# Probabilities times values in full fp32 on half the TensorE columns, in a hybrid decoder trunk

## The chip, the core and the metric

The kernel runs on one core of a Trainium2 chip. The metric is device time in microseconds (us) of one execution. A profile is one execution taken by the hardware profiler, with the same kernel; its times carry the names and lines of the kernel's code.

## What is computed

Two decoder layers over 512 tokens of width 1024. The first layer is a convolution module and a SwiGLU feed-forward part; then one shared set of keys and values is projected; the second layer is sliding-window attention over them and a second feed-forward part. Cut to the attention, where `probs` times `v_band` is what the change touches:

```python
def banded_sink_attention(q, k, v, sinks, rel_bias):
    # 16 query heads, 4 key/value heads of 64, 4 blocks of 128 queries;
    # a block sees its own 128 keys and the 128 before
    s = jnp.einsum('bnqhgd,bnkhd->bnhgqk', qb, k_band) * (HEAD_DIM ** -0.5)
    s = jnp.where(mask, s + bias, NEG_INF)
    m = jnp.maximum(jnp.max(s, axis=-1, keepdims=True), sink)
    p = jnp.exp(s - m)
    probs = p / (jnp.sum(p, axis=-1, keepdims=True) + jnp.exp(sink - m))
    o = jnp.einsum('bnhgqk,bnkhd->bnqhgd', probs, v_band)
    return o.reshape(B, S, N_HEADS * HEAD_DIM)
```

## The kernel before

Activations lie with features on the 128 partitions and tokens along the free dimension. Weights come in pieces of 128 x 1024 floats, in the order of a plan written out at the start: DMA on the SP queue (line 188), then ScalarE writes a rounded high part (`whi`, line 204) and VectorE the rest (`wlo`, line 205). `mm3` (lines 259 to 265) multiplies two such split operands with three matmuls in the fp32r type: high times high, high times low, low times high. The first projection (line 630) alone multiplies unsplit fp32 tiles, of 256 columns.

Around the attention the work stands like this. While the last of layer 0's feed-forward part runs, the normalised inputs of keys, values and queries are made. `kq` takes the keys, split. The values come out of the banks `vb`, 128 tokens at a time, are scaled by the token's norm (line 980), and are split into two tiles `vq` that were set to zero by two memsets on GpSimd (line 950). In `vq` each pair of key/value heads has four slots of 64 columns, [v0, 0, 0, v1]: slots 0 and 1 are the first side's values with zeros beside them, slots 2 and 3 are zeros with the second side's values.

`unit` is the attention of one pair of key/value heads (`gp`), one half of their query heads (`jp`) and one block of 128 queries (`n`); there are 16 units, of one key block (n = 0) or two. A unit has these steps, parted by `yield`:

- scores (line 1024): 12 matmuls, alternately with the upper and the lower 64 rows of the array, into two banks; one small matmul (line 1019) stands ahead of them so that they are issued in that order; VectorE adds the bias and takes the extreme (line 1027);
- exponentials on ScalarE (line 1034), a reciprocal on VectorE (line 1036), the scaling on GpSimd (line 1038);
- for each key block four transposes on TensorE into a bank (line 1046), from which ScalarE writes the high part `pth` (line 1049) and VectorE the rest `ptl` (line 1050);
- probabilities times values, P·V (lines 1053 to 1059): for each key block and each side `g` one `mm3` of 256 columns into the bank `po`. Its stationary operand is 128 columns of `vq`, one side's 64 and the zeros, so the two sides add up in one accumulation over all 128 partitions: 6 matmuls per key block, 168 in all, on lines 263 to 265;
- `po` is split into the output tiles (lines 1064 and 1065).

`pipeline` staggers the units, and its steps are set between the matmuls of the query projections (`query`) and of the first half of the output projection. On top of that a scheduler that simulates the engines' times decides the order in which each engine gets its instructions, so the order in the code isn't that of the engines: a P·V group may stand broken up between projections and transposes.

Tiles come from rotating pools: 8 banks of PSUM; 11 wide buffers `quad`, of which `vq` holds two; two each of `pth` and `ptl`.

Of the kernel before, what the change touches and what calls it, by code (L numbers as in the profile page):

```python
# [10 lines left out]
F32 = mybir.dt.float32  # L11
F32R = mybir.dt.float32r
AF = mybir.ActivationFunctionType
ALU = mybir.AluOpType
# [3 lines left out]
P = 128  # L18
# [8 lines left out]
HD = 64  # L27
NBLK = S // P
BAND = 2 * P
# [121 lines left out]
def hybrid_trunk(ctx: ExitStack, tc: tile.TileContext, xT, W, prm_in, wdw_in, sinks, relb, onehot, fin, out):  # L151
    nc = tc.nc
    cpool = ctx.enter_context(tc.tile_pool(name="const", bufs=1))
    quads = ctx.enter_context(tc.tile_pool(name="quads", bufs=11))
# [8 lines left out]
    def uid(s):  # L163
        ctr[0] += 1
        return f"{s}{ctr[0]}"

    def bank():
        return ps.tile([P, 512], F32, tag="bank", name=uid("bank"))

    def quad(dt=F32R):  # L170
        return quads.tile([P, 4, 512], dt, tag="quad", name=uid("quad"))

    def temp():
        return tmp.tile([P, 512], F32, tag="tmp", name=uid("tmp"))

    def f32(ap):
        return ap.bitcast(F32)
# [81 lines left out]
    def mm3(out, w, x, start, stop):  # L259
        if w[1] is None:  # L260
            nc.tensor.matmul(out, w[0], x, start=start, stop=stop)
            return
        nc.tensor.matmul(out, w[0], x[0], start=start, stop=False)  # L263
        nc.tensor.matmul(out, w[0], x[1], start=False, stop=False)  # L264
        nc.tensor.matmul(out, w[1], x[0], start=False, stop=stop)  # L265
# [141 lines left out]
    def split(dst, src):  # L407
        nc.scalar.copy(dst[0], src)  # L408
        nc.vector.tensor_sub(dst[1], src, f32(dst[0]))
# [504 lines left out]
    at = attn.enter_context(tc.tile_pool(name="attn", bufs=2))  # L914
# [25 lines left out]
    if True:  # L940
# [4 lines left out]

        xkv = x["kv"]
        kq = quads.tile([P, 2, 2, 512], F32R, tag="quad", name="kq")
        vq = [quads.tile([P, 4, 2, 4, HD], F32R, tag="quad", name=uid("vq")) for _ in range(2)]
        for v in vq:
            nc.gpsimd.memset(f32(v), 0.0)  # L950
        kb = [bank() for _ in range(2)]
        for half in range(2):
            whi, wlo = get("kv", 0, half)
# [6 lines left out]
        vb = [bank() for _ in range(4)]  # L960
        for half in range(2):
# [7 lines left out]
            if half == 0:  # L969
                rs_bc = rms.step2()  # L970
                rs = rms.rs
                for m in range(2):
                    t = temp()
# [2 lines left out]
        flush()  # L976
        rate[0] = 0
        for n in range(4):
            t = temp()
            nc.vector.tensor_scalar(t[:, 0:256], vb[n][:, 0:256], rs[:, n:n + 1], None, op0=ALU.mult)  # L980
            split([v[:, n, :, 0:4:3, :] for v in vq], t[:, 0:256].rearrange("p (a g c) -> p a g c", a=2, g=2))

        qs, os_ = {}, {}

# [21 lines left out]
        def unit(gp, jp, n):  # L1006
            qt = slice(n * P, (n + 1) * P)
            k0 = max(n - 1, 0) * P
            nk = 1 if n == 0 else 2
            w = nk * P  # L1010
            rows = [slice(HD * g, HD * (g + 1)) for g in range(2)]
            heads = [gp * 8 + g * 4 + 2 * jp + e for g in range(2) for e in range(2)]
            sc = at.tile([P, 4, 1 + BAND], F32, tag="sc", name=uid("sc"), bufs=3)
            sinks4 = sk.rearrange("p (a g j e) -> p a g j e", a=2, g=2, j=2)[:, gp, :, jp, :]
            nc.gpsimd.tensor_copy(sc[:, :, 0].rearrange("p (g e) -> p g e", g=2), sinks4)
            m4 = small.tile([P, 4], F32, tag="m4", name=uid("m4"))
            pbs = [bank().rearrange("p (a b) -> p a b", a=2) for _ in range(2)]

            mm = nc.tensor.matmul(pbs[1][0:1, 0, 0:1], ones_c, ones_c, start=True, stop=True)
            for e in range(2):  # L1020
                for a, b in ((0, 0), (0, 1), (1, 0)):
                    for g in range(2):
                        with tc.issue_after(mm.ins):
                            mm = nc.tensor.matmul(pbs[g][:, e, :], qs[gp, jp][rows[g], 2 * a + e, qt],  # L1024
                                                  kq[rows[g], b, gp, k0:k0 + BAND], start=a + b == 0, stop=a == 1)
            for u, hd in enumerate(heads):
                nc.vector.tensor_tensor_reduce(
                    sc[:, u, 1:1 + w], pbs[u // 2][:, u % 2, 0:w], bias[:, hd, BAND - w:BAND],
                    op0=ALU.add, op1=ALU.min, scale=1.0, scalar=sk[:, hd:hd + 1],
                    accum_out=m4[:, u:u + 1])  # L1030
            yield
            sm = small.tile([P, 4], F32, tag="sm", name=uid("sm"))
            for j in range(4):
                nc.scalar.activation(sc[:, j, 0:1 + w], sc[:, j, 0:1 + w], AF.Exp, bias=m4[:, j:j + 1],
                                     scale=-1.0, accum_out=sm[:, j:j + 1])
            nc.vector.reciprocal(sm, sm)  # L1036
            for j in range(4):
                nc.gpsimd.tensor_scalar(sc[:, j, 1:1 + w], sc[:, j, 1:1 + w], sm[:, j:j + 1], 0.0,  # L1038
                                        op0=ALU.mult, op1=ALU.add)
            yield  # L1040
            yield
            pts = []
            for kb_ in range(nk):
                pt = bank()
                for j in range(4):
                    nc.tensor.transpose(pt[:, j * P:(j + 1) * P], sc[:, j, 1 + kb_ * P:1 + (kb_ + 1) * P], ident)  # L1046
                hi = at.tile([P, 512], F32R, tag="pth", name=uid("pth"), bufs=2)
                lo = at.tile([P, 512], F32R, tag="ptl", name=uid("ptl"), bufs=2)
                nc.scalar.copy(hi, pt)
                nc.vector.tensor_sub(lo, pt, f32(hi))  # L1050
                pts.append((hi, lo))
            yield
            po = bank()[:, 0:BAND]
            for kb_ in range(nk):
                blk = k0 // P + kb_
                for g in range(2):
                    vs = [v[:, blk, gp, 2 * g:2 * g + 2, :].rearrange("p a c -> p (a c)") for v in vq]
                    mm3(po, vs, [pt[:, g * BAND:(g + 1) * BAND] for pt in pts[kb_]],
                        kb_ == 0 and g == 0, kb_ == nk - 1 and g == 1)
            if n == 0:  # L1060
                os_[gp, jp] = quad()
            hi, lo = (os_[gp, jp][:, 2 * a:2 * a + 2, qt] for a in range(2))
            src = po.rearrange("p (j q) -> p j q", j=2)
            nc.scalar.copy(hi, src)
            nc.vector.tensor_sub(lo, src, f32(hi))
            yield

        def pipeline():
            units = [unit(gp, jp, n) for gp in range(2) for jp in range(2) for n in range(NBLK)]
            for t in range(len(units) + 4):  # L1070
                for d in (4, 3, 1, 0):
                    if 0 <= t - d < len(units):
                        next(units[t - d])
                        if d == 1:
                            next(units[t - d])
                yield
# [129 lines left out]
```

## Time and profile before

| | |
|---|---|
| median of 3 runs | 1104.37 us (1103.89 to 1104.98) |
| the profiled execution | 1105.28 us, span of its instructions 1103.5 us |
| mean granted TensorE clock | 0.995 of full speed |
| TensorE matmuls busy | 1088.4 us, 99% of the span |
| TensorE weight loads busy | 931.5 us, 84% |
| VectorE, ScalarE, GpSimd busy | 662.7, 506.1, 335.3 us |

In the profile PE is TensorE's matmuls, PEld its weight loads, DVE is VectorE, ACT ScalarE, POOL GpSimd, SP the engine whose queue issues most DMAs. A row of a group gives line, engine, operation, output and inputs by the program's names, shape, count; then busy time in us and the mean ns of one; then the engine's idle time ahead of them and what ended it. Durations of matmuls include the pipeline's latency, so in a dense stream they overlap, and the distance from start to start is what one costs. An fp32 matmul is shown as two pieces.

### The profile page before, as it was taken

Reading aid. Unit: us, or ns where it says so; the run is one execution under the profiler, and the core shown is the slowest. Engines: PE = TensorE matmul, PEld = TensorE weight load, DVE = VectorE, ACT = ScalarE, POOL = GpSimd, SP = SyncE. Lnnn points to the kernel's source line nnn. Section 1 sums busy time; section 2 is a strip of 40 time slices with the busy share of each in tenths; the row PEclk is TensorE's granted clock in tenths of the full one; section 3 lists DMA queues with packets and bytes.
Section 4 is the critical chain, followed back from the end, with each engine's and each line's share of the span. In section 5 each row is a group of like instructions: output and inputs, shape, how many; then the busy total and the mean of one; then the engine's idle time right before and its main releaser. Section 6 shows DMA issues by size and latency. Waiting matters only on the chain.

```text
span 1103.5 us, 15186 instructions
## 1 busy us (share of the span) xinstructions
PE 1088.4 (99%) x5680; PEld 931.5 (84%) x5680; DVE 662.7 (60%) x1077; ACT 506.1 (46%) x914; POOL 335.3 (30%) x433
## 2 busy tenths in 40 slices
PE   8999998999999999999999999999999999999997
PEld 7888888999988888888888788888888888888886
DVE  3999989977777544443565777584453333444353
ACT  3887887764665333232353765453332211232233
POOL 3999999610322111111220342131111100111010
PEclk9999998999999999999999999999999999999999
DMA  9218044475455422222223111122222222222212
GB/s 359 108 23 93 17 166 152 166 253 185 176 187 191 153 96 93 98 96 96 96 77 114 59 39 41 56 96 112 98 85 107 96 96 96 96 96 96 96 39 76
DMA packets 39557, 123.37 MB, mean 112 GB/s; under 512 B 4251, under 2 KB 11068, under 8 KB 39484
## 3 DMA queue, kind: packets, MB, share of 16 engines
q1 hardware_dynamic: 38476, 121.19, 32.7%
q10 hardware_dynamic: 1008, 1.23, 0.3%
q8 instruction: 44, 0.72, 0.3%
q14 instruction: 29, 0.24, 0.1%
HBM read 117.15 MB, written 5.24 MB: 111 GB/s over the span
## 4 chain that ended last, share of the span: by engine, by line
PE 87%; DVE 5%; issue 3%; ACT 3%; POOL 1%; DMA 0%; SPq 0%; POOLq 0%; DVEq 0%
PE bank L264 22%; PE bank L263 22%; PE bank L265 22%; PE bank L630 9%; PE bank L295 5%; PE bank L296 3%; DVE bank L679 2%; PE bank L1136 1%; PE bank L1024 1%; DVE quad L405 1%; PE bank L1046 1%; ACT pr L671 1%; DVE wlo L205 1%; POOL pr L672 1%; PE bank L728 1%
## 5 line engine op out<-in xcount | busy, mean ns | idle before, releaser
L264 PE MATMUL bank<-quad,whi 128*128 128x512 f32 (+1 forms) x1232 | 449.6, 365 | 2.8 <-DVE quad L405 2.8
L265 PE MATMUL bank<-quad,wlo 128*128 128x512 f32 (+1 forms) x1232 | 448.8, 364 | 2.1 <-DVE wlo L205 2.1
L263 PE MATMUL bank<-quad,whi 128*128 128x512 f32 (+1 forms) x1232 | 449.9, 366 | 0.0
L205 DVE TENSOR_TENSOR wlo<-raw,whi 128x1024 fp32r<-128x1024 f32 x190 | 265.3, 1397 | 296.1 <-ACT whi L204 291.8
L204 ACT CAST whi<-raw 128x1024 fp32r<-128x1024 f32 x190 | 199.2, 1049 | 325.0 <-PE bank L264 272.2
L264 PEld LDWEIGHTS bank<-quad,whi 128*128 128x128 f32 x1232 | 233.6, 190 | 40.8 <-DVE quad L405 3.9
L265 PEld LDWEIGHTS bank<-quad,wlo 128*128 128x128 f32 x1232 | 233.6, 190 | 38.7 <-DVE wlo L205 2.5
L263 PEld LDWEIGHTS bank<-quad,whi 128*128 128x128 f32 x1232 | 233.5, 190 | 37.5 <-issue 0.5
L534 POOL TENSOR_TENSOR tmp<-tmp,tmp 128x512 f32<-128x512 f32 x34 | 48.1, 1417 | 408.8 <-DVE tmp L533 393.5
L672 POOL TENSOR_TENSOR pr<-pr,pr 128x256 f32<-128x256 f32 x208 | 157.8, 794 | 1.6 <-ACT pr L671 1.6
L630 PE MATMUL bank<-quad,w 128*128 128x256 f32 x512 | 114.4, 383 | 2.3 <-DVE quad L605 1.3
L679 DVE SCALAR_TENSOR_TENSOR bank<-apad,wdw,bank 128x256 f32<-128x256 f32 x248 | 112.8, 485 | 3.4
L630 PEld LDWEIGHTS bank<-quad,w 128*128 128x128 f32 x512 | 98.0, 192 | 16.7 <-DVE quad L605 2.9
L671 ACT ACTIVATE pr<-apad,wdw 128x256 f32<-128x256 f32 x208 | 99.2, 502 | 20.2 <-POOL pr L672 18.6
L362 POOL TENSOR_TENSOR tmp<-tmp,tmp 128x256 f32<-128x256 f32 (+1 forms) x35 | 37.9, 1082 | 152.8 <-ACT tmp L358 123.4
L295 PE MATMUL bank<-quad,whi 128*128 128x512 f32 x212 | 75.9, 398 | 0.0
L532 ACT ACTIVATE tmp<-tmp 128x512 f32<-128x512 f32 x34 | 21.4, 632 | 93.0 <-DVE tmp L531 93.0
L296 PE MATMUL bank<-quad,wlo 128*128 128x256 f32 x212 | 59.3, 280 | 0.0
L1038 POOL TENSOR_SCALAR sc<-sc,sm 128x256 f32<-128x256 f32 (+1 forms) x64 | 31.9, 517 | 73.8 <-DVE sm L1036 65.7
L295 PEld LDWEIGHTS bank<-quad,whi 128*128 128x128 f32 x212 | 39.7, 188 | 8.4
L533 DVE TENSOR_TENSOR tmp<-bank,rsbc 128x512 f32<-128x512 f32 x34 | 23.5, 691 | 32.4 <-PE bank L265 32.4
L408 ACT CAST quad<-tmp 128x512 fp32r<-128x512 f32 (+1 forms) x50 | 29.2, 585 | 29.4 <-POOL tmp L534 26.6
(165 smaller groups left out, 982.1 us busy)
## 6 DMA issues: line engine op xcount, KB each, us to landing
raw<-in_W_dram SPq DMA_DIRECT2D x198, 512.0 KB, 3.5
w<-in_W_dram SPq DMA_DIRECT2D x15, 512.0 KB, 9.7
fd<-fs SPq DMA_DIRECT2D x1, 3072.0 KB, 33.8
h<-in_xT_dram SPq DMA_DIRECT2D x8, 256.0 KB, 6.4
bias<-fd SPq DMA_DIRECT2D x8, 256.0 KB, 5.7
out_dram<-hg SPq DMA_DIRECT2D x3, 256.0 KB, 2.1
out_dram<-hg ACTq DMA_DIRECT2D x3, 256.0 KB, 2.3
w<-in_W_dram SPq DMA_DIRECT2D x2, 256.0 KB, 4.9
```

The lines of the kernel that those rows point to most:

```text
L204: nc.scalar.copy(hi, r)
L205: lo_engine[0].tensor_sub(lo, r, f32(hi))
L263: nc.tensor.matmul(out, w[0], x[0], start=start, stop=False)
L264: nc.tensor.matmul(out, w[0], x[1], start=False, stop=False)
L265: nc.tensor.matmul(out, w[1], x[0], start=False, stop=stop)
L295: nc.tensor.matmul(first[2], first[0], first[1], start=start, stop=False)
L296: nc.tensor.matmul(second[2], second[0], second[1], start=False, stop=stop)
L534: nc.gpsimd.tensor_mul(t2, t1, t2)
L630: mm = nc.tensor.matmul(self.pb[:, w * W2:(w + 1) * W2], w1[ct][:, w, k, :], x[k] if x else xg[k][:, tok], start=k == 0, stop=k == KT - 1)
L671: on_act = nc.scalar.mul(pr, a[:, j:j + W2], tap(j))
L672: on_pool = nc.gpsimd.tensor_add(pr, acc, pr)
L679: on_dve = nc.vector.scalar_tensor_tensor(yt if i == nd - 1 else c, src, tap(i), c if i else self.shift, op0=ALU.mult, op1=ALU.add)
```

## The change

The values are kept as plain fp32, 64 columns to a side, with no zeros: `vq` is one tile, written straight from the bank by the scaling. The transposed probabilities are copied out of their bank once, as fp32, by ScalarE for a unit's first key block and VectorE for its second. P·V is one fp32 matmul for each key block and side, with 64 stationary columns, written to that side's own 64 partitions of `po`: the first side uses columns 0 to 63 of the array, the second 64 to 127 (in the program, tiles of 128 rows x 64 columns). It is 56 matmuls in all. The new copies rotate over three buffers.

```diff
@@ keys and values
         kq = quads.tile([P, 2, 2, 512], F32R, tag="quad", name="kq")
-        vq = [quads.tile([P, 4, 2, 4, HD], F32R, tag="quad", name=uid("vq")) for _ in range(2)]
-        for v in vq:
-            nc.gpsimd.memset(f32(v), 0.0)
+        vq = quads.tile([P, 4, 2, 2, HD], F32, tag="quad", name=uid("vq"))
...
         for n in range(4):
-            t = temp()
-            nc.vector.tensor_scalar(t[:, 0:256], vb[n][:, 0:256], rs[:, n:n + 1], None, op0=ALU.mult)
-            split([v[:, n, :, 0:4:3, :] for v in vq], t[:, 0:256].rearrange("p (a g c) -> p a g c", a=2, g=2))
+            nc.vector.tensor_scalar(vq[:, n].rearrange("p a g c -> p (a g c)"), vb[n][:, 0:256], rs[:, n:n + 1], None,
+                                    op0=ALU.mult)
@@ unit
-                hi = at.tile([P, 512], F32R, tag="pth", name=uid("pth"), bufs=2)
-                lo = at.tile([P, 512], F32R, tag="ptl", name=uid("ptl"), bufs=2)
-                nc.scalar.copy(hi, pt)
-                nc.vector.tensor_sub(lo, pt, f32(hi))
-                pts.append((hi, lo))
+                pr = at.tile([P, 512], F32, tag="prt", name=uid("prt"), bufs=3)
+                (nc.vector.tensor_copy if kb_ else nc.scalar.copy)(pr, pt)
+                pts.append(pr)
             yield
             po = bank()[:, 0:BAND]
             for kb_ in range(nk):
                 blk = k0 // P + kb_
                 for g in range(2):
-                    vs = [v[:, blk, gp, 2 * g:2 * g + 2, :].rearrange("p a c -> p (a c)") for v in vq]
-                    mm3(po, vs, [pt[:, g * BAND:(g + 1) * BAND] for pt in pts[kb_]],
-                        kb_ == 0 and g == 0, kb_ == nk - 1 and g == 1)
+                    nc.tensor.matmul(po[g * HD:(g + 1) * HD, :], vq[:, blk, gp, g, :], pts[kb_][:, g * BAND:(g + 1) * BAND],
+                                     start=kb_ == 0, stop=kb_ == nk - 1)
```

## The prediction

> **What bounds the kernel now.** I read the engine totals and the chain that ended last, then the stage that the edit touches in the view by stretches, then its groups of instructions, then TensorE's timeline there.
>
> ```profile
> PE 1088.4 (99%) x5680; PEld 931.5 (84%) x5680; DVE 662.7 (60%) x1077; ACT 506.1 (46%) x914; POOL 335.3 (30%) x433
> PE 87%; DVE 5%; issue 3%; ACT 3%; POOL 1%; DMA 0%; SPq 0%; POOLq 0%; DVEq 0%
> ```
> ```profile
> 577.00:605.00 28.00, 28.00 (x176) 24.72 (x176) 16.43 (x25) 9.36 (x14) 1.02 (x1) 1.00 0.29 95
> 605.00:640.00 35.00, 35.00 (x236) 27.76 (x235) 24.31 (x78) 22.78 (x67) 12.63 (x28) 1.00 0.17 61
> 640.00:680.00 40.00, 40.00 (x269) 33.60 (x267) 27.70 (x79) 24.45 (x71) 14.02 (x30) 1.00 0.15 53
> 680.00:717.00 37.00, 37.00 (x254) 32.26 (x255) 22.91 (x62) 18.78 (x54) 7.39 (x19) 1.00 0.13 45
> ```
>
> Each row is a stretch: its length, then the busy time of PE, weight loads, DVE, ACT and POOL, then PE's granted clock. Attention runs from about 605 to 717 us, the values are projected and stored before it. PE is busy through all of every stretch at full clock, DVE for 23 to 28 us of 35 to 40. So what decides is time on PE; a saving on DVE, ACT or POOL is worth something only if PE waits for it.
>
> ```profile
> L263 PE MATMUL bank<-pth,vq 128*128 128x256 f32 x56 | 16.0, 286 | 0.0
> L264 PE MATMUL bank<-ptl,vq 128*128 128x256 f32 x56 | 16.8, 300 | 0.0
> L265 PE MATMUL bank<-pth,vq 128*128 128x256 f32 x56 | 15.7, 281 | 0.0
> L263 PEld LDWEIGHTS bank<-pth,vq 128*128 128x128 f32 x56 | 10.5, 188 | 1.0 <-ACT pth L1049 0.2
> L1050 DVE TENSOR_TENSOR ptl<-bank,pth 128x512 fp32r<-128x512 f32 x28 | 18.7, 686 | 4.4 <-ACT pth L1049 4.1
> L1049 ACT CAST pth<-bank 128x512 fp32r<-128x512 f32 x28 | 15.8, 586 | 3.2 <-PE bank L1046 1.7 <-PE bank L265 0.8
> L630 PE MATMUL bank<-quad,w 128*128 128x256 f32 x512 | 114.4, 383 | 2.3 <-DVE quad L605 1.3 <-DMA w<-in_W_dram 1.1
> L1024 PE MATMUL bank<-kq,quad 64*128 64x256 f32 x192 | 16.4, 298 | 0.0
> L1019 PE MATMUL bank<-ones_c 128*1 128x1 f32 x32 | 3.0, 164 | 0.0
> ```
>
> The first three rows are what the edit replaces: 56 x 3 = 168 matmuls of 256 columns, with no idle time before them. A mean of 281 to 300 ns is latency, not what a matmul costs in a stream; that is read from starts in the timeline (start, duration):
>
> ```profile
> 647.68 0.60 PE L1046 MATMUL bank<-ident,sc 128*128 128x128 f32 x4
> 648.03 0.49 PE L264 MATMUL bank<-quad,whi 128*128 128x512 f32 x1
> 648.36 0.28 PE L264 MATMUL bank<-ptl,vq 128*128 128x256 f32 x1
> 648.48 0.28 PE L265 MATMUL bank<-pth,vq 128*128 128x256 f32 x1
> 648.59 0.28 PE L263 MATMUL bank<-pth,vq 128*128 128x256 f32 x1
> 648.71 0.28 PE L264 MATMUL bank<-ptl,vq 128*128 128x256 f32 x1
> 648.83 0.29 PE L265 MATMUL bank<-pth,vq 128*128 128x256 f32 x1
> 648.95 0.60 PE L1046 MATMUL bank<-ident,sc 128*128 128x128 f32 x4
> 649.48 0.19 PE L1019 MATMUL bank<-ones_c 128*1 128x1 f32 x2
> 649.60 0.96 PE L1024 MATMUL bank<-kq,quad 64*128 64x256 f32 x12
> 650.50 0.50 PE L265 MATMUL bank<-quad,wlo 128*128 128x512 f32 x1
> 650.84 0.40 PE L263 MATMUL bank<-quad,whi 128*128 128x512 f32 x1
> 651.08 0.40 PE L264 MATMUL bank<-quad,whi 128*128 128x512 f32 x1
> ```
>
> **Removed on PE.** Five P·V matmuls start from 648.36 on and the next work at 648.95: 0.59 / 5 = 0.118 us each. 168 x 0.118 = 19.8 us go.
>
> **Added on PE.** 56 matmuls in full fp32 with 256 columns and 64 weight columns. The nearest row is the first projection, fp32 with 256 columns: L630 is 256 matmuls in the code (16 calls x 2 halves x 8 slices) and 512 in the row, so each is two, and 114.4 / 512 = 0.223 us per piece. 112 pieces one after the other take 25.0 us.
>
> The two sides stand on different column halves of the array, so they may run at once. The nearest row is L1024: its matmuls alternate between two row halves, and 12 of them take 0.90 us (649.60 to 650.50), where 12 in turn would take 12 x 0.118 = 1.42. Six pairs take 0.71, the remaining 0.19 is dealt with below. No row shows two column halves, but I take them to overlap as the row halves do. In order, a side's two pieces follow each other on one half, so only the second piece of one side runs beside the first of the next: two matmuls take three piece times, four take five. In the order of the changed program on PE the 56 stand in 23 groups, 18 of two and 5 of four: 18 x 3 + 5 x 5 = 79 piece times, 17.6 us. Full overlap would be 12.5, none 25.0.
>
> The Trainium skill ("TensorE: Matmul & The Clock Gate", Part 3, measured speedup) gives three column tiles 2.38 times the speed; as an estimate, 79% of the ideal makes two tiles 1.59 times as fast, 15.7 us. No run here shows it; by it the sum below would be 1.9 us lower.
>
> **Changes of the array's shape.** This is the term that speaks against the change. Going into L1019 (a tile of 32 columns), four transposes take 0.53 us (648.95 to 649.48); the four before took 0.68 with one 512-column matmul of about 0.24, so 0.44: 0.09 lost. Coming back after L1024, the first 512-column matmul takes 0.34 to the next start (650.50 to 650.84) against 0.24 right after: 0.10 lost, its weights not loaded ahead. The 0.19 left in L1024 is the same pair: 0.10 at its first piece, 0.09 at its end. So a change of shape costs 0.09 (draining) to 0.19 us (draining and the first load). In the order of the programs, TensorE changes shape 60 times in attention before and 100 times after: 46 borders of the 23 groups come, and 6 others go as the row groups are broken less. 40 x 0.19 = 7.6 us; with draining alone 3.6. I take 0.19, since both ways across L1024 show both parts.
>
> **Off PE.** Nothing in these is on the path.
>
> ```profile
> L950 POOL MEMSET vq<- 128x2048 f32 x2 | 3.6, 1824 | 3.8 <-PE bank L264 3.8
> L409 DVE TENSOR_TENSOR vq<-tmp,vq 128x256 fp32r<-128x256 f32 x4 | 1.5, 417 | 0.0
> L408 ACT CAST vq<-tmp 128x256 fp32r<-128x256 f32 x4 | 1.5, 404 | 1.9 <-DVE tmp L980 1.9
> ```
>
> The memsets (3.6 us) and the splitting of the values (1.5 us each on ACT and DVE) go; PE is full from 577 to 605 on other matmuls, so nothing is gained. In attention 28 subtractions (18.7 us of DVE) go and 12 DVE copies of the same size come, 7.0 to 8.2 us by the ACT copy's 586 ns and the subtraction's 686; ACT loses 16 x 586 ns = 9.4 us. The weight-load row of P·V shows 0.2 us of waiting on pth in all, so I cost this at nothing: the cover is other matmuls standing between copy and use, and if it were gone PE would wait at most one copy, 0.6 to 0.7 us, a few times. No new wait holds a queue: the copies stand where the old ones stood, DMAs keep their order, and one wide buffer fewer can only free transfers earlier, for a PE that waits for none.
>
> **Sum.** −19.8 + 17.6 + 7.6 = +5.4 us. The profiled execution took 1105.28 us (span 1103.5); it becomes 1110.7. The median of the runs, 1104.37, is 0.9 lower: 1109.8.
>
> **Rivals.**
> *The sides don't overlap, two pieces after another throughout.* Against it L1024's halves; for it, that no row has two column halves, and both share the same 128 rows. −19.8 + 25.0 + 7.6 = +12.8: 1117.2.
> *They overlap fully.* This needs one side's two pieces to pass each other, which in-order starts speak against: +0.3: 1104.7.
> *Column shape without a price (faster).* If TensorE passes between the whole array and 64-column tiles without draining, the 46 borders cost nothing and the 6 fewer others save 1.1: −19.8 + 17.6 − 1.1 = −3.3: 1101.1. It decides once a change of shape costs under 2.2 / 40 = 0.055 us. Against it, L1019 is a column tile and shows the 0.09.
> *No splitting at all* (the halves run as the whole array, no borders): −19.8 + 25.0 − 1.1 = +4.1: 1108.5. Against: the program gives them tiles of 64 columns.
> *Weights not loaded ahead in column tiles.* In a stream a load runs beside the matmul before:
>
> ```profile
> 648.36 0.19 PEld L265 LDWEIGHTS bank<-pth,vq 128*128 128x128 f32 x1
> ```
>
> This one starts with the L264 matmul at 648.36, 0.12 before its own. If every one of the 112 pieces paid the 0.10 us seen after a change of shape, and ran alone: 112 x 0.323 + 7.6 − 19.8 = +24.0: 1128.4. The Trainium skill's rule (same page, Part 3, what overlaps and what doesn't) is that loads overlap running matmuls only when the row group differs, which both column halves share. By that rule this rival would hold; the row above, whole array behind whole array, does not agree with it.
>
> **How the numbers follow.** Forecast 0.45, no overlap 0.22, full overlap 0.09, no price 0.11, no splitting 0.07, no load ahead 0.06. Leaving out the last and the faster one (0.17) gives 1104.0 to 1118.5: from just under full overlap to just over none; draining alone (4.0 us less, 1105.8) lies inside. A measurement of this kernel tells about 0.2%, 2.2 us. Faster by more: the no-price case, 0.11. Within: full overlap and the low edge of the others, 0.13. Slower: the rest, 0.76.
>
> **What would show it.** In the changed profile: 112 P·V pieces on 64 columns; in a group of two, starts at 0, 0.22 (and the other side's first at almost the same time), then 0.45, which is right, or four starts 0.22 apart, which is no overlap. The work after a group 0.09 late, and the next step 0.10 longer. PE still without idle time from 605 on, and attention ending some 5 us later. The forecast is wrong if attention's end moves by under 2 or over 10 us, or if the time comes from outside attention.

## The result, and the profile after

The changed kernel is faster by a little, not slower: 1102.26 us against 1104.53 (medians of 18 runs each), ratio 0.9981, 95% interval 0.9974 to 0.9987. The prediction had 1109.8 and a range from 1104.0.

From the page of the changed kernel: the span, the engine totals and the head of the chain that ended last.

```profile
span 1100.1 us, 15008 instructions
PE 1086.0 (99%) x5624; PEld 914.0 (83%) x5624; DVE 651.7 (59%) x1057; ACT 499.6 (45%) x898; POOL 335.8 (31%) x431
PE 86%; DVE 5%; issue 3%; ACT 3%; POOL 1%; DMA 1%; SPq 0%; POOLq 0%; DVEq 0%
```

DVE is 11 us less busy, ACT 6.5, and PE is as full as before: it still decides. The stretches of attention in the changed kernel (columns as in the prediction):

```profile
577.00:603.50 26.50, 26.50 (x164) 23.35 (x166) 13.72 (x19) 7.65 (x10) 1.02 (x1) 1.00 0.31 100
603.50:640.00 36.50, 36.50 (x236) 25.59 (x236) 23.32 (x79) 23.60 (x71) 12.73 (x28) 1.00 0.17 58
640.00:680.00 40.00, 40.00 (x262) 28.27 (x259) 24.77 (x77) 22.72 (x69) 17.29 (x34) 1.00 0.15 54
680.00:714.00 34.00, 34.00 (x209) 24.20 (x208) 18.48 (x47) 14.80 (x39) 7.18 (x16) 1.00 0.13 48
```

The two profiled executions differ by more than the medians do: 3.4 us of span. Of this 1.4 us is there before the first attention matmul and has nothing to do with the change. PE's instructions are the same, in the same order, up to the first P·V, and the difference arises in the first 12 us. There PE stood idle for 1.5 us of 7 in the execution of before and for 0.8 in that of after, and the one was granted 0.76 of the clock, the other all of it. First the row of before, then that of after:

```profile
5.00:12.00 7.00, 5.47 (x17) 4.28 (x18) 3.77 (x6) 2.13 (x6) 4.19 (x7) 0.76 1.05 372
```
```profile
5.00:12.00 7.00, 6.16 (x24) 4.16 (x25) 3.13 (x6) 2.17 (x6) 4.73 (x7) 1.00 1.06 368
```

The clock is not the whole of it. The fifth piece of the first projection starts 1.25 us later in the execution of before, behind a longer wait for VectorE, which had itself waited for the DMA of `h`; up to 7.3 us its clock was still at 1.00, and from 7.3 to 10.8 at 0.51. Before, then after:

```profile
7.63 5.68 PE L630 MATMUL bank<-quad,w 128*128 128x256 f32 x18 [1.26 <-DVE quad L605]
```
```profile
6.38 1.13 PE L630 MATMUL bank<-quad,w 128*128 128x256 f32 x4 [0.23 <-DVE quad L605]
```

The other 2.0 us are gained between 603 us and the end of P·V, and they agree with the 2.3 us of the medians. PE's timeline of the changed kernel around two groups (start, duration):

```profile
638.84 0.39 PE L265 MATMUL bank<-quad,wlo 128*128 128x512 f32 x1
639.15 1.08 PE L1052 MATMUL bank<-prt,vq 128*64 128x256 f32 x8
640.17 0.66 PE L1043 MATMUL bank<-ident,sc 128*128 128x128 f32 x4
640.75 0.19 PE L1016 MATMUL bank<-ones_c 128*1 128x1 f32 x2
645.32 0.39 PE L263 MATMUL bank<-quad,whi 128*128 128x512 f32 x1
645.64 0.65 PE L1052 MATMUL bank<-prt,vq 128*64 128x256 f32 x4
646.23 1.09 PE L1043 MATMUL bank<-ident,sc 128*128 128x128 f32 x8
```

Four P·V matmuls are eight pieces here. From 639.15 to 640.17 they take 1.02 us; two matmuls, four pieces, take 0.59 (645.64 to 646.23). In the starts, not merged as here, the eight pieces stand at 0, 6, 266, 273, 482, 489, 698 and 705 ns: four pairs, 6 ns apart within a pair, and 216 ns from pair to pair once the first is past. The four pieces are two such pairs. So a group of two matmuls takes two piece times and a group of four takes four, where the prediction counted three and five (0.67 and 1.12 us of pieces alone); the 0.16 us left in each group is the price of going into and out of the shape.

To see where the time went I summed, for each kind of matmul, the distance from its start to the next start on PE, from the first one-column matmul to just past the last P·V:

| kind of matmul | before | after |
|---|---|---|
| P·V | 168 in 21.9 us | 112 pieces in 15.6 us |
| transposes | 112 in 12.9 us | 112 in 15.2 us |
| projections, 512 columns | 239.6 ns each | 247.1 ns each (for 256 of them 1.9 us more) |
| scores and the one-column matmuls | 17.0 us | 17.0 us |

P·V gained 6.4 us and its neighbours lost 4.2, their part of the price of the array's changes of shape. That leaves 2.1 us.

### The profile page after: what moved, and what is told of

Same layout as the page of the kernel before. It is cut to its first block, busy times and chain, and to the rows that moved or that the text cites. A ratio compares the mean times of both kernels' runs of the same rounds, so it can differ in the third digit from the quotient of the medians.

```text
span 1100.1 us, 15008 instructions
## 1 busy us (share of the span) xinstructions
PE 1086.0 (99%) x5624; PEld 914.0 (83%) x5624; DVE 651.7 (59%) x1057; ACT 499.6 (45%) x898; POOL 335.8 (31%) x431
## 4 chain that ended last, share of the span: by engine, by line
PE 86%; DVE 5%; issue 3%; ACT 3%; POOL 1%; DMA 1%; SPq 0%; POOLq 0%; DVEq 0%
PE bank L263 21%; PE bank L264 21%; PE bank L265 21%; PE bank L630 8%; PE bank L295 5%; PE bank L296 3%; DVE bank L679 2%; PE bank L1130 1%; PE bank L1052 1%; PE bank L1043 1%; PE bank L1021 1%; DVE wlo L205 1%; DVE quad L405 1%; ACT pr L671 1%; POOL pr L672 1%
## 5 line engine op out<-in xcount | busy, mean ns | idle before, releaser
L1035 POOL TENSOR_SCALAR sc<-sc,sm 128x256 f32<-128x256 f32 (+1 forms) x64 | 34.2, 553 | 67.7 <-DVE sm L1033 67.7
```

## The experiments

The question was where the gain came from, and why the two sides overlap fully although each side's two pieces are issued one behind the other.

**The zeros put back, all else changed.** This keeps the fp32 copies and goes without the splits, as the changed kernel does; it brings back one of the two memsets, and it takes away the halves.

```diff
-        vq = quads.tile([P, 4, 2, 2, HD], F32, tag="quad", name=uid("vq"))
+        vq = quads.tile([P, 4, 2, 4, HD], F32, tag="quad", name=uid("vq"))
+        nc.gpsimd.memset(vq, 0.0)
...
-                    nc.tensor.matmul(po[g * HD:(g + 1) * HD, :], vq[:, blk, gp, g, :], pts[kb_][:, g * BAND:(g + 1) * BAND],
-                                     start=kb_ == 0, stop=kb_ == nk - 1)
+                    nc.tensor.matmul(po, vq[:, blk, gp, 2 * g:2 * g + 2, :].rearrange("p a c -> p (a c)"),
+                                     pts[kb_][:, g * BAND:(g + 1) * BAND],
+                                     start=kb_ == 0 and g == 0, stop=kb_ == nk - 1 and g == 1)
```

> The changed kernel with the zeros put back beside the values (one fp32 tile, one memset of it), so each P·V matmul is fp32 over all 128 columns and the sides add up in one accumulation as before. All that the change does off PE stays. Theory A (the gain is PE time from the halves running at once): 112 pieces of 0.216 us in turn, 24.2 us instead of the 21.9 us that P·V steps took before, and no change of shape for P·V: 2 to 4 us slower than before, ratio 1.002 to 1.004. Theory B (the gain comes from the relief of DVE, ACT and GpSimd): this kernel has that relief too and is faster than before by about the 2 us of the change.

Measured: 1107.77 us, ratio to before 1.0029 (1.0018 to 1.0041). In its timeline four pieces on the whole array take 0.86 us to the next start:

```profile
628.06 0.39 PE L263 MATMUL bank<-quad,whi 128*128 128x512 f32 x1
628.29 1.02 PE L1053 MATMUL bank<-prt,vq 128*128 128x256 f32 x4
629.15 0.27 PE L1044 MATMUL bank<-ident,sc 128*128 128x128 f32 x1
```

The matmul ahead of them takes 0.23 us, so nothing is lost at the border. Theory A holds. Full fp32 alone makes the kernel slower, and the relief of DVE, ACT and GpSimd, which this kernel has as well but for one memset, brings nothing that shows. What makes the change a gain is the halves running at once.

**Both sides on the same half.** The second side's matmuls go to columns 0 to 63 of a second bank, and its rows are evacuated from there.

```diff
-            po = bank()[:, 0:BAND]
+            pos = [bank()[:, 0:BAND] for _ in range(2)]
...
-                    nc.tensor.matmul(po[g * HD:(g + 1) * HD, :], vq[:, blk, gp, g, :], ...
+                    nc.tensor.matmul(pos[g][0:HD, :], vq[:, blk, gp, g, :], ...
...
```

> The changed kernel with both sides of P·V on columns 0 to 63, each in a bank of its own, and each side's rows evacuated separately. Theory A1 (each column half takes its own pieces in turn, and a side's first piece need not wait for the other side's second): nothing overlaps, starts 0.21 us apart, 112 x 0.21 = 23.5 us instead of 11.7, about 11 us slower than the changed kernel, ratio to before about 1.008. Theory A2 (the two pieces of one fp32 matmul run at once, side after side): starts still come in pairs 6 ns apart and the time is that of the changed kernel within 2 us.

Measured: 1113.49 us, ratio 1.0081 (1.0065 to 1.0096), so 11 us above the changed kernel. One group of two matmuls in its timeline:

```profile
627.77 0.39 PE L263 MATMUL bank<-quad,whi 128*128 128x512 f32 x1
628.09 1.08 PE L1052 MATMUL bank<-prt,vq 128*64 128x256 f32 x4
629.10 0.33 PE L1043 MATMUL bank<-ident,sc 128*128 128x128 f32 x1
```

Four pieces take 1.01 us where they took 0.59; their starts stand at 0, 266, 482 and 698 ns. P·V's distances add up to 27.2 us instead of 15.6. The border ahead of the group (0.32 instead of 0.23) is as with two halves. So two pieces on one half do not run at once here, and A2 falls. PE waits for nothing in this kernel's attention, so the separate evacuations are not what costs the time. The prediction's rival of no overlap had +12.8 us by its sum; the kernel that really lacks it stands 9 us above the kernel before.

**One side's matmuls ahead of the other's.** Both this kernel and the next issue a unit's second key block first and the rest of its P·V behind it, so that most units run in one go.

```diff
-            for kb_ in range(nk):
-                blk = k0 // P + kb_
-                for g in range(2):
-                    nc.tensor.matmul(...
-                                     start=kb_ == 0, stop=kb_ == nk - 1)
+            mm = None
+            for g in range(2):
+                for kb_ in reversed(range(nk)):
+                    blk = k0 // P + kb_
+                    with tc.issue_after(mm.ins) if mm else nullcontext():
+                        mm = nc.tensor.matmul(...
+                                              start=kb_ == nk - 1, stop=kb_ == 0)
```

> The changed kernel with a unit's P·V kept together: the second key block first and the rest issued behind it, and both key blocks of one side ahead of those of the other. Theory A1 with a reach of at least four pieces: eight pieces of a unit still start in four pairs 6 ns apart, 0.21 us from pair to pair; time as in the kernel that keeps a unit together with the sides in turn, 1 to 3 us faster than the changed kernel. Order kept (a piece starts only after all issued before it): seven piece times instead of four for twelve units, 12 x 3 x 0.21 = 7.6 us slower than that kernel.

Measured: 1102.47 us, ratio 0.9981 (0.9972 to 0.9990). In a unit issued in one go, four pieces of one side stand ahead of four of the other, and still they run in pairs. From its timeline:

```profile
628.75 1.09 PE L1054 MATMUL bank<-prt,vq 128*64 128x256 f32 x8
629.77 0.66 PE L1043 MATMUL bank<-ident,sc 128*128 128x128 f32 x4
681.85 0.65 PE L1054 MATMUL bank<-prt,vq 128*64 128x256 f32 x2
682.43 0.44 PE L1043 MATMUL bank<-ident,sc 128*128 128x128 f32 x2
```

Eight pieces take 1.02 us, as with the sides in turn; the starts are 13 ns apart in a pair instead of 6. The order-kept theory had seven piece times, 1.5 us. The trace does not name the side of a piece, so the order of issue is inferred, and the distance within a pair speaks for it: 3 to 4 ns for two scores on the two row halves, issued one right behind the other; 6 to 7 with the sides of P·V in turn, where one piece of the first side is issued between the two; 13 to 14 here, where three are. That is some 3.3 ns for each piece issued.

The last two rows are one of two units that the scheduler broke up: a single matmul's two pieces take 0.58 us with nothing on the other half to run beside them, as much as four pieces take otherwise. That is part of why this kernel is not the 1 to 3 us faster than the changed one that was expected (P·V's distances add up to 15.7 us, in the next kernel to 14.8); the other part is the wait told of next, which it has too.

**A unit's P·V kept together.** The same with the sides in turn (`for g` inside).

> The changed kernel with a unit's P·V kept together: the second key block first and the rest issued behind it, sides in turn. TensorE changes shape 88 times in attention instead of 100. If a change of shape costs 0.17 us each, as the borders of the changed kernel's P·V groups do on average, it is 12 x 0.17 = 2.0 us faster than the changed kernel, ratio to before about 0.996. If the price lies only in the first weight load, part of which a longer group hides, under 1 us, ratio about 0.9975.

Measured: 1101.23 us, ratio 0.9971 (0.9960 to 0.9981); 1.1 us off the changed kernel by the ratios, between the two cases. The intervals of the two kernels overlap (the changed one's is 0.9974 to 0.9987), so the size of this step is not firm. A group of its profile, and its timeline, show why it isn't 2.0:

```profile
L1054 PE MATMUL bank<-prt,vq 128*64 128x256 f32 x112 | 16.1, 396 | 1.1 <-DVE prt L1045 1.1
```
```profile
704.17 1.09 PE L1043 MATMUL bank<-ident,sc 128*128 128x128 f32 x8
706.32 1.08 PE L1054 MATMUL bank<-prt,vq 128*64 128x256 f32 x8 [1.06 <-DVE prt L1045]
```

The order put one unit's P·V right behind the last transposes, with no other matmuls between, and PE waited 1.1 us for the copy. It is the cover that the prediction named, gone at one place, and it cost more than the one copy of 0.6 to 0.7 us that the prediction allowed: VectorE had another instruction of 0.42 us first (L1062), then the copy of 0.68. Without the wait it would be 2.2 us for 12 changes of shape; that figure is worked out, not measured.

**P·V beside the scores.** A unit's P·V is kept together as in the kernel above (that part of the edit is not shown again). It now comes behind the transposes and right ahead of the next unit's scores, so in 12 of the 16 units the array goes from 64-column tiles to the scores' shapes without passing through the whole array.

```diff
-                pr = at.tile([P, 512], F32, tag="prt", name=uid("prt"), bufs=3)
+                pr = at.tile([P, 512], F32, tag="prt", name=uid("prt"), bufs=4)
...
-                for d in (4, 3, 1, 0):
+                for d in (3, 1, 4, 0):
```

> A unit's P·V kept together and put right ahead of the next unit's scores, behind the transposes (four buffers for the transposed probabilities instead of three). TensorE changes shape 76 times in attention: 24 fewer than in the changed kernel, 12 fewer than with P·V kept together alone, which took 1.1 us off the changed kernel (ratio 0.9971 against 0.9981). By 0.09 us for each change saved, as there, ratio to before about 0.996; by 0.17, about 0.994. Rival: P·V now stands nearer to the copies that it reads, TensorE waits for them, and the ratio is 0.997 or more.

Measured: 1098.39 us, ratio 0.9949 (0.9937 to 0.9962), the fastest of all: 5.6 us off the kernel before and 3.5 off the changed one by the ratios. If all of this is put down to the 24 changes of shape fewer, it is 0.15 us each. Its timeline at one unit, and its group of P·V:

```profile
644.40 1.03 PE L1043 MATMUL bank<-ident,sc 128*128 128x128 f32 x8
645.36 0.65 PE L1054 MATMUL bank<-prt,vq 128*64 128x256 f32 x4
645.95 0.19 PE L1016 MATMUL bank<-ones_c 128*1 128x1 f32 x2
646.07 0.97 PE L1021 MATMUL bank<-kq,quad 64*128 64x256 f32 x12
646.96 0.50 PE L263 MATMUL bank<-quad,whi 128*128 128x512 f32 x1
```
```profile
L1054 PE MATMUL bank<-prt,vq 128*64 128x256 f32 x112 | 15.6, 394 | 0.0
```

Transposes, P·V, scores and projection follow one another, and P·V has no idle time before it.

**The same without the one-column matmul.**

```diff
-            mm = nc.tensor.matmul(pbs[1][0:1, 0, 0:1], ones_c, ones_c, start=True, stop=True)
+            mm = None
...
-                        with tc.issue_after(mm.ins):
+                        with tc.issue_after(mm.ins) if mm else nullcontext():
```

> As the kernel with P·V beside the scores, without the one-column matmul ahead of each unit's scores (it only sets the order of issue; no output needs it). TensorE changes shape 69 times, and 16 small matmuls go (32 pieces of 26 ns, and the change into and out of their 32-column shape). By 0.09 to 0.17 us for each change saved and 0.8 us for the pieces, 1.4 to 2 us faster than with it. Rival: without it the scores' first matmuls are issued in ones and twos between transposes and P·V, each with a change of shape and no partner on the other row half, and it is no faster.

Measured: 1098.91 us, ratio 0.9951 (0.9938 to 0.9965): no faster, as the rival had it. The scores' group, in this kernel and in the one with the small matmul:

```profile
L1021 PE MATMUL bank<-kq,quad 64*128 64x256 f32 x192 | 18.6, 302 | 0.0
```
```profile
L1021 PE MATMUL bank<-kq,quad 64*128 64x256 f32 x192 | 16.4, 298 | 0.0
```

The scores are busy for 2.2 us longer on PE. By starts it is 1.8 us, which is about what the one-column matmuls had taken (1.9). Some first matmuls are issued alone, ahead of projections, and run without a partner on the other row half:

```profile
623.39 0.38 PE L1021 MATMUL bank<-kq,quad 64*128 64x256 f32 x1
623.70 0.50 PE L263 MATMUL bank<-quad,whi 128*128 128x512 f32 x1
```

## Why the prediction was wrong

**The step that failed** is the overlap of the halves, the term +17.6. It let only the second piece of one side run beside the first piece of the next, because starts would keep the order of issue. The runs show that pieces keep turn on a half, not across the halves: a piece starts when its own half is free, even ahead of pieces issued before it for the other half. Even four pieces in a row for one side don't hold up the other. So 112 pieces take 56 x 0.216 = 12.1 us, 5.5 less. That is the rival of full overlap, which had 0.09 of the chances, at 1104.7. Against it stood only that in-order starts speak against it, and the prediction showed no row for that. Its nearest row, L1024, couldn't tell: its matmuls are one piece each and the halves already alternate in the order of issue.

**The second step** is the price of the changes of shape. With the overlap alone mended the sum is −19.8 + 12.1 + 7.6 = −0.1, 1104.3, still inside the range; the measured time is 2 us lower. With P·V's removed time and the pieces as they are, the −2.1 us of the table leaves 5.6 for the net 40 changes of shape, 0.14 each instead of 0.19. The starts of the changed kernel bear that out. Going into P·V costs 0.09 at the matmul ahead and 0.05 at the first pair. Leaving it costs 0.10 at the last pair and 0.06 at a first transpose, or 0.11 at a first projection: 0.14 in, 0.16 or 0.21 out, and 19 of the 23 groups go out to transposes. The prediction had taken the 0.19 from the scores' borders, with 0.10 for every first load.

**A term that was a little off.** By distances P·V took 21.9 us before, not 19.8. 0.118 us is the step inside a run of P·V matmuls; in 13 places one stood first behind the one-column matmul or the scores, or last ahead of them, and took 0.21 to 0.22. The prediction's sum holds that time too, in its net count of the changes, and so do the 5.6 us.

**Where it was right.** PE decides, and the time saved off PE counts for nothing: the kernel with the zeros put back shows that. A change of shape has a price and it eats most of the gain: taking 24 of them away gives 3.5 us more. A piece takes 0.22 us. The faster rival (1101.1) is nearer to the measured time than any other and had the right sign, but by luck: the changes of shape are not free, they were paid from a larger gain.

**The rival on weight loads** is refuted. In the changed kernel four loads of a group take place in its first 0.20 us, while only two of the pieces have started (the third starts at 0.27):

```profile
645.64 0.20 PEld L1052 LDWEIGHTS bank<-prt,vq 128*64 128x64 f32 x4 [0.35 <-ACT sc L1031]
```

The Trainium skill's rule cited for it ("TensorE: Matmul & The Clock Gate", Part 3, what overlaps and what doesn't), loads beside running matmuls only with another row group, does not agree with this row: both column halves share all rows. Its figure for three column tiles, 2.38 times, gave the prediction an estimate of 1.59 times for two. Here two halves reach 2.0 times inside a group, a pair every 216 ns where the same half takes one piece in that time.

## What to carry to other kernels

An operand padded with zeros to fill the array can be worth replacing by two half-width matmuls on different columns: here their pieces ran in half the time, in both orders of issue that were tried. But count how often the array changes between whole, row-split and column-split tiles, at 0.14 to 0.21 us a change here, and put split work next to other split work; that gave more (3.5 us) than the change itself (2.3). When a trace shows two matmuls overlap, ask whether the order of issue in that row could have shown the opposite.

## What the runs showed of the hardware that I had not expected

- The column halves of the array start fp32 pieces independently of each other: pairs 6 ns apart with the sides in turn, 13 ns with four pieces of one side issued ahead of four of the other. How far this reaches beyond four pieces was not tried.
- A change to 64-column tiles loses less at the first piece than one to row halves or back: the first distance within P·V is 266 ns against 216 after it, 50 ns, while the first pair of scores takes 220 ns against about 115; a first 512-column matmul after P·V loses about 0.11 us (337 ns to the next start against 227), as it does after the scores (338).
- The first 12 us moved the profiled span by 1.4 us between two executions of the same PE instructions, more than half of the effect measured here. Both a longer wait (1.26 against 0.23 us) and the granted clock (0.76 against 1.00) differed there; how much each made was not separated.
